# Feed-forward output projections in two halves of the tokens: 256-column matmuls and two evacuations in place of 512-column matmuls and one

## The chip, the cores and the metric

The kernel runs on one core of one Trainium2 chip. The metric is the device time of one execution in microseconds (us), the median of the runs that are shown.

## The reference, cut to what matters

The model is a trunk of two layers on 512 tokens of width 1024, all in float32. Each layer is a half-weighted feed-forward block, a mixer (Mamba-2 SSD in layer 0, S5 in layer 1) and a second half-weighted feed-forward block. The change touches the four feed-forward blocks alone:

```
def swiglu(h, w_in, w_out):
    gate, up = jnp.split(h @ w_in, 2, axis=-1)
    return (jax.nn.silu(gate) * up) @ w_out

x = x + 0.5 * swiglu(rmsnorm(x, ffn1_norm[i]), ffn1_w_in[i], ffn1_w_out[i])
...
x = x + 0.5 * swiglu(rmsnorm(x, ffn2_norm[i]), ffn2_w_in[i], ffn2_w_out[i])
```

`w_in` is 1024 x 5632 and `w_out` 2816 x 1024, so the hidden width is 2816, which is 22 tiles of 128.

## The kernel before, in words

**Layout.** Activations are kept with channels on the partitions and the 512 tokens along the free axis: `xT[d]`, d = 0 to 7, are eight tiles of 128 x 512 in float32. Six stages run one after the other: `f1_0`, `ssd`, `f2_0`, `f1_1`, `s5`, `f2_1`; the four whose names begin with f are the feed-forward blocks.

**Three matmuls per product.** To keep float32 accuracy with the fast matmul type F32R, each operand is split into a rounded part and a rest. Weights go through `load_w` (L186): a DMA into `wst`, a ScalarE cast into `whi` (L194) and a VectorE subtraction into `wlo` (L196). `proj` (L199) then issues three matmuls for each of its contraction tiles, and each of them names its own 128 x 128 stationary block, so each matmul in the profile has a weight load (engine PEld) of its own:

```
for k in range(n):
    PE.matmul(ps, hi[:, k], H[k], start=first and k == 0, stop=False)       # L203
    PE.matmul(ps, hi[:, k], L[k], start=False, stop=False)                  # L204
    PE.matmul(ps, lo[:, k], H[k], start=False, stop=last and k == n - 1)    # L205
```

**A feed-forward stage, `ffn` (L208).** The 22 hidden tiles are worked in three parts of 8, 7 and 7. For each hidden tile of a part, `proj` computes the gate and the up product, each into a PSUM bank of its own (`mm`, 4 banks in turn). VectorE scales both (`gt` L225, `up` L228), ScalarE applies silu (L226), VectorE multiplies (L229), and the result is split again: `ah` by ScalarE (L231), `al` by VectorE (L233). When a part is done, its output projection follows: for each of the eight output tiles d, `proj` contracts the 8 or 7 tiles `ah`, `al` with the weights of that part into one bank, in 24 or 21 matmuls of 512 columns, and one VectorE instruction (L240) adds half of the bank to `xT[d]`. In the third part, `nxt.take(d)` then prepares the operand of the next stage from `xT[d]` (L170, L172, L157, L162). So a stage has 8 x 22 x 3 = 528 matmuls in output projections and the program 2112.

**What sets the order.** In the feed-forward stages a scheduler places the instructions of each engine; each engine then runs its own list in that order and waits at an instruction until its operands are there. In `ssd` and `s5`, TensorE keeps the order in which the code was written. `fill` hands a feed-forward stage small pieces of other work (the set-up of S5), one after each tile. Buffers that the text speaks of: four banks of the name `mm`, four more of the name `aux`, four `wst`, three each of `whi` and `wlo`, eight each of `ah` and `al`.

Of the kernel before, what the change touches and what calls it, by code (L numbers as in the profile page):

```python
# [30 lines left out]
def trunk_kernel(ctx, tc, x, ffn1_norm, ffn1_w_in, ffn1_w_out, mix_norm, ffn2_norm, ffn2_w_in, ffn2_w_out,  # L31
# [31 lines left out]
    # token residues: qsel[t, (c, q)] = (t % 8 == q), kmask[t, k] = (t // 8 == k)  # L63
# [49 lines left out]
    def newton_rsqrt(ps4, n, scale):  # L113
        """rsqrt(ps4*scale + eps) on a small tile of n columns"""
        v = work.tile([128, 16], F32, name="nw_v")[:, :n]
        hv = work.tile([128, 16], F32, name="nw_h")[:, :n]
        y = work.tile([128, 16], F32, name="nw_y")[:, :n]
        a = work.tile([128, 16], F32, name="nw_a")[:, :n]
        V.tensor_scalar(v, ps4, scale, EPS, op0=OP.mult, op1=OP.add)
        V.tensor_scalar(hv, v, -0.5, None, op0=OP.mult)  # L120
        V.tensor_scalar(a.bitcast(I32), v.bitcast(I32), 1, None, op0=OP.logical_shift_right)
        V.tensor_scalar(y.bitcast(I32), a.bitcast(I32), -1, 0x5f3759df, op0=OP.mult, op1=OP.add)
        for _ in range(3):
            V.tensor_tensor(a, y, y, op=OP.mult)
            V.tensor_tensor(a, a, hv, op=OP.mult)
            V.scalar_tensor_tensor(y, a, 1.5, y, op0=OP.add, op1=OP.mult)
        return y

    def compact_sum(accs, p=None, first=True, last=True):
        """[128, 512] tiles -> sum over partitions and tiles, [128 t, 4]"""  # L130
        p = p or aux_ps()
        for i, acc in enumerate(accs):
            for c in range(4):
                for q in range(4):
                    PE.matmul(p[q * 32:(q + 1) * 32, c:c + 1], acc[:, c * 128 + q * 32:c * 128 + q * 32 + 32],  # L135
                              ones[:, 0:1], start=first and i == 0 and c == 0, stop=last and i == len(accs) - 1,
                              skip_group_check=True)
        return p

    def bcast_rows(y4):  # L140
        """[128 t, 4] -> psum [128, 512], the same row on every partition"""
        p = aux_ps()
        for c in range(4):
            PE.transpose(p[:, c * 128:(c + 1) * 128], y4[:, c:c + 1].to_broadcast([128, 128]), ident)
        return p

    class Prep:
        """takes finished x tiles and prepares the operand of the next stage"""
# [37 lines left out]
    def load_w(src, kt, eng=None):  # L186
        """src [kt*128 rows, 128 columns] -> exact hi/lo stationary blocks"""
        st = wpool.tile([128, KD, 128], F32, name="wst", bufs=4)[:, :kt]
        (eng or nc.sync).dma_start(st, src.rearrange("(k p) c -> p k c", p=128))
        return split_w(st, kt)  # L190
# [17 lines left out]
    def ffn(pr, w_in, w_out, nxt, fill=()):  # L208
        fill = list(fill)

        def pop():
            if fill:
                fill.pop(0)()

        with tc.tile_pool(name="ffn", bufs=2) as fp:
            for a, b in PARTS:
                AH, AL = [], []
                for f in range(a, b):
                    pg, pu = mm_ps(), mm_ps()
                    wg = load_w(w_in[:, f * 128:(f + 1) * 128], KD)  # L220
                    proj(pg, wg, pr.H, pr.L)
                    wu = load_w(w_in[:, FF + f * 128:FF + (f + 1) * 128], KD)
                    proj(pu, wu, pr.H, pr.L)
                    gt = fp.tile([128, T], F32, name="gt")
                    V.tensor_tensor(gt, pg, pr.rbc, op=OP.mult)  # L225
                    S.activation(gt, gt, AF.Silu)  # L226
                    up = fp.tile([128, T], F32, name="up")
                    V.tensor_tensor(up, pu, pr.rbc, op=OP.mult)  # L228
                    V.tensor_tensor(up, up, gt, op=OP.mult)  # L229
                    ah = fp.tile([128, T], F32R, name="ah", bufs=8)  # L230
                    S.copy(ah, up)  # L231
                    al = fp.tile([128, T], F32R, name="al", bufs=8)
                    V.tensor_tensor(al, up, ah.bitcast(F32), op=OP.subtract)  # L233
                    AH.append(ah)
                    AL.append(al)
                    pop()
                for d in range(KD):
                    po = mm_ps()
                    proj(po, load_w(w_out[a * 128:b * 128, d * 128:(d + 1) * 128], b - a), AH, AL)
                    V.scalar_tensor_tensor(xT[d], po, 0.5, xT[d], op0=OP.mult, op1=OP.add)  # L240
                    if b == FT:
                        nxt.take(d)
                    pop()
            while fill:
                fill.pop(0)()
        nxt.finish()

# [1 line left out]
    def ssd(pr, nxt):  # L249
        w_in, w_out = ssd_in_proj[0], ssd_out_proj[0]  # L250
        with ExitStack() as es:
            sc = es.enter_context(tc.tile_pool(name="ssdc", bufs=1))
            sp = es.enter_context(tc.tile_pool(name="ssd", bufs=2))
            # dt for the 32 heads, on four quadrants
# [74 lines left out]
            def conv(ct):  # L329
                """conv channel tile ct (of 32), silu'd, feature-major"""  # L330
# [25 lines left out]
            def out_rows(a, b, last=False):  # L356
                """adds the product of inner tiles a..b with their rows of the output weights"""
                for d in range(KD):
                    po = mm_ps()
                    proj(po, load_w(w_out[a * 128:b * 128, d * 128:(d + 1) * 128], b - a), YH[a:b], YL[a:b])  # L360
                    V.tensor_tensor(xT[d], po, xT[d], op=OP.add)
                    if last:
                        nxt.take(d)
                    pop()
# [10 lines left out]
            def scan(g, BT, CT, XS, SZ):  # L375
                """pieces of the scan of one group"""
                st = {}

                def head():
                    # chunk products C.B, token-major operands  # L380
# [47 lines left out]
                def decay(e):  # L428
                    # decays inside the chunks, per head
# [14 lines left out]
                def outp(e):  # L444
                    M = st["M", e]
                    # decay from the states, rows per head pair
# [80 lines left out]
    s5 = {}  # L527

    def s5_setup(pp, part):
        """closures that build the S5 operators in DRAM"""  # L530
        # per 8 groups: input, state-output and in-chunk operators; phase tables
# [13 lines left out]
        def expf(o, src):  # L545
            """exp to float32 accuracy, argument held to [-87, 88]"""
# [36 lines left out]
        def load_bc(i):  # L583
            gs = slice(i * 8, i * 8 + 8)
            # B stacks: [re; im] and [-im; re]
# [5 lines left out]
            # C stacks: [re; im] and [im; re]  # L591
# [9 lines left out]
        def load_d():  # L601
            # skip term
# [13 lines left out]
        def lam():  # L616
# [22 lines left out]
            # expm1(a) = 2t/(1+|t|) * max(1, e^a), t = tanh(a/2)  # L639
# [6 lines left out]
            # powers of lambda_bar, m = 0..8  # L646
# [22 lines left out]
            # c0 = (lambda_bar - 1)/lambda  # L669
# [25 lines left out]
            # |lambda_bar|^8 and the unit phase ^8, conjugated on the lower half  # L695
# [27 lines left out]
            # [re; -re], [-im; -im]  # L723
# [5 lines left out]
        def tables(i):  # L729
            """phase tables for 8 groups: cos, sin of k times the phase of 8 steps"""  # L730
# [18 lines left out]
        def ops(i):  # L749
            """input and output operators of 4 groups"""  # L750
# [82 lines left out]
    def s5_sink(d, g):  # L833
        """x*gain of a finished tile, tokens as (q, k), to DRAM"""
# [10 lines left out]
    def in_ops(i):  # L845
        """tokens of 8 groups, their input operators and tables"""
# [11 lines left out]
    def out_ops(i, h):  # L858
        """output operators of 4 groups"""
        if (i, h) not in s5_out:  # L860
            P_ = s5["op"].tile([128, 4, 256], F32, name="opP", bufs=5)
            nc.sync.dma_start(P_, s5["P"][:, i * 8 + h * 4:i * 8 + h * 4 + 4])
            s5_out[i, h] = P_
        return s5_out[i, h]
# [8 lines left out]
    def res_w(j):  # L873
        """weights kept whole while the scan runs, in the tiles of the next operand"""
# [9 lines left out]
    def s5_stage(pr, nxt):  # L884
        with ExitStack() as es:
            sp = es.enter_context(tc.tile_pool(name="s5", bufs=2))
            # 1/rms in the (c, q) x k layout
# [10 lines left out]
            def scan(i):  # L898
                """states before every chunk, rotated back"""
# [30 lines left out]
            def mix(i, ins, gy):  # L930
                """outputs of tiles i and i + 1, (tile, k) x (g, q, c)"""
# [11 lines left out]
            def channels(i, gy):  # L943
                """back to channels x (q, k)"""
# [169 lines left out]
```

## Time and profile before

| | |
|---|---|
| time, median of 2 runs | 2126.34 us (2125.13 and 2127.54) |
| span of the profiled execution | 2124.6 us |
| TensorE matmul busy | 2055.0 us (97%), 10755 records |
| VectorE busy | 1256.6 us (59%) |
| ScalarE busy | 793.7 us (37%) |
| DMA, mean | 108 GB/s |
| mean granted TensorE clock | 0.987 |

The profiled execution's span is 1.7 us below the median, and what lies around a span is not in it. PE is TensorE's matmul row, PEld its weight loads, which overlap the matmuls; DVE is VectorE, ACT ScalarE, POOL GpSimd, SP the queue that issues most DMAs. A matmul's row gives the time from its start to its modelled end, and the next one starts before that end, so the distance between two starts, not the row's duration, is what a matmul costs in a row of them; below it is called the step. A matmul on plain float32 operands shows as two records in the trace, one of type F32R as one. "L203 PE MATMUL mm<-ah,whi 128*128 128x512" is a matmul at line 203 that writes `mm` from the moving tile `ah` and the stationary tile `whi`, with 512 columns.

### The profile page before, as it was taken

How to read it: one execution, taken by the hardware profiler on the slowest of the kernel's cores; microseconds unless marked ns; L12 is line 12 of the kernel's file. 1: busy time of each engine (PE TensorE's matmuls, PEld its weight loads, DVE VectorE, ACT ScalarE, POOL GpSimd, SP SyncE). 2: the span in 40 equal slices, each digit the busy share in tenths (PEclk: the TensorE clock that was granted, in tenths of full speed). 3: DMA queues.
4: the chain of work that ended last, by engine and by line, in shares of the span. 5: the costliest groups of instructions: out<-in, count | busy, mean ns of one | idle time of the engine just before them, and what ended most of it. 6: DMA issues, size and time to landing. Idle time of an engine off the chain costs nothing.

```text
span 2124.6 us, 27175 instructions
## 1 busy us (share of the span) xinstructions
PE 2055.0 (97%) x10755; PEld 1691.2 (80%) x10755; DVE 1256.6 (59%) x2171; ACT 793.7 (37%) x1146; POOL 44.9 (2%) x116
## 2 busy tenths in 40 slices
PE   6999999999999999699999999999996999999997
PEld 5888888888888887587788888888885788888886
DVE  6887445678875787477844454344457654434444
ACT  4223223566753664243422333232254433222222
POOL 1000000000000001000000000000001000000000
PEclk9999999999999999899999999999998999999999
DMA  5344333322223214756533363333357233332331
GB/s 153 110 130 138 91 99 83 99 74 76 70 72 91 77 41 117 123 148 174 154 95 100 94 201 92 99 96 99 95 159 244 83 100 89 99 100 81 108 92 58
DMA packets 408672, 228.50 MB, mean 108 GB/s; under 512 B 45656, under 2 KB 397072, under 8 KB 408544
## 3 DMA queue, kind: packets, MB, share of 16 engines
q1 hardware_dynamic: 383120, 200.24, 33.1%
q0 software_dynamic: 4272, 13.66, 2.8%
q10 hardware_dynamic: 21152, 12.86, 2.1%
q8 instruction: 84, 1.38, 0.3%
q14 instruction: 44, 0.36, 0.1%
HBM read 204.64 MB, written 22.09 MB: 107 GB/s over the span
## 4 chain that ended last, share of the span: by engine, by line
PE 93%; DVE 3%; DMA 2%; ACT 1%; issue 1%; SPq 0%; POOL 0%; ACTq 0%; DVEq 0%
PE mm L203 29%; PE mm L205 29%; PE mm L204 29%; DMA p_B<-in_s_b_re_dram 1%; PE aux L464 1%; PE aux L414 0%; DVE z L919 0%; PE aux L457 0%; DMA wst<-in_ffn_w_in_dram 0%; PE aux L434 0%; DMA p_lrow<-in_s_lam_re_dram 0%; PE aux L135 0%; PE aux L204 0%; PE aux L205 0%; PE aux L203 0%
## 5 line engine op out<-in xcount | busy, mean ns | idle before, releaser
L194 ACT CAST whi<-wst 128x1024 fp32r<-128x1024 f32 (+2 forms) x357 | 361.1, 1013 | 953.6 <-PE mm L204 676.2
L203 PE MATMUL mm<-hH,whi 128*128 128x512 f32 x1800 | 706.4, 393 | 1.2 <-DVE gt L225 1.2
L205 PE MATMUL mm<-hH,wlo 128*128 128x512 f32 x1800 | 703.5, 391 | 0.0
L204 PE MATMUL mm<-hL,whi 128*128 128x512 f32 x1800 | 703.0, 391 | 0.0
L196 DVE TENSOR_TENSOR wlo<-wst,whi 128x1024 fp32r<-128x1024 f32 (+2 forms) x357 | 418.8, 1174 | 107.9 <-ACT whi L194 104.1
L203 PEld LDWEIGHTS mm<-hH,whi 128*128 128x128 f32 x1800 | 339.2, 189 | 73.1 <-issue 2.0
L205 PEld LDWEIGHTS mm<-hH,wlo 128*128 128x128 f32 x1800 | 338.8, 188 | 71.3 <-issue 0.4
L204 PEld LDWEIGHTS mm<-hL,whi 128*128 128x128 f32 x1800 | 339.1, 188 | 69.8
L204 PE MATMUL mm<-al,whi 128*128 128x512 f32 x704 | 275.8, 392 | 0.0
L205 PE MATMUL mm<-ah,wlo 128*128 128x512 f32 x704 | 275.3, 391 | 0.0
L203 PE MATMUL mm<-ah,whi 128*128 128x512 f32 x704 | 274.9, 391 | 0.0
L228 DVE TENSOR_TENSOR up<-mm,rbc 128x512 f32<-128x512 f32 x88 | 60.7, 690 | 222.2 <-PE mm L205 222.1
L240 DVE SCALAR_TENSOR_TENSOR xT<-mm,xT 128x512 f32<-128x512 f32 x96 | 66.1, 689 | 197.6 <-PE mm L205 197.6
L204 PEld LDWEIGHTS mm<-al,whi 128*128 128x128 f32 x704 | 132.1, 188 | 28.7 <-issue 0.2
L205 PEld LDWEIGHTS mm<-ah,wlo 128*128 128x128 f32 x704 | 132.1, 188 | 28.6 <-issue 0.2
L203 PEld LDWEIGHTS mm<-ah,whi 128*128 128x128 f32 x704 | 132.1, 188 | 28.3
L225 DVE TENSOR_TENSOR gt<-mm,rbc 128x512 f32<-128x512 f32 x88 | 60.7, 690 | 154.8 <-PE mm L205 149.4
L231 ACT CAST ah<-up 128x512 fp32r<-128x512 f32 x88 | 54.8, 623 | 66.3 <-DVE up L229 66.2
L340 DVE SCALAR_TENSOR_TENSOR cv<-raw,cols,cv 128x512 f32<-128x512 f32 x96 | 70.9, 745 | 0.7
L229 DVE TENSOR_TENSOR up<-up,gt 128x512 f32<-128x512 f32 x88 | 60.7, 690 | 7.8 <-ACT gt L226 0.7
L226 ACT ACTIVATE gt<-gt 128x512 f32<-128x512 f32 x88 | 55.1, 627 | 17.0 <-DMA d_P<-p_ks 13.2
L233 DVE TENSOR_TENSOR al<-up,ah 128x512 fp32r<-128x512 f32 x88 | 60.1, 684 | 1.4 <-ACT ah L231 1.4
(333 smaller groups left out, 1726.0 us busy)
## 6 DMA issues: line engine op xcount, KB each, us to landing
wst<-in_ffn_w_in_dram SPq DMA_DIRECT2D x176, 512.0 KB, 3.9
wst<-in_ffn_w_out_dram SPq DMA_DIRECT2D x64, 448.0 KB, 3.7
wst<-in_ssd_in_proj_dram SPq DMA_DIRECT2D x48, 512.0 KB, 4.0
wst<-in_ffn_w_out_dram SPq DMA_DIRECT2D x32, 512.0 KB, 4.2
opP<-d_P SPq DMA_DIRECT2D x16, 512.0 KB, 5.0
wst<-in_s_glu_w_dram POOLq DMA_DIRECT2D x12, 512.0 KB, 5.2
d_t<-p_cs POOLq DMA_DIRECT2D x8, 512.0 KB, 3.0
wst<-in_ssd_out_proj_dram SPq DMA_DIRECT2D x8, 512.0 KB, 4.1
```

Source lines behind the costliest of these rows:

```text
L194: S.copy(hi, st)
L196: V.tensor_tensor(lo, st, hi.bitcast(F32), op=OP.subtract)
L203: PE.matmul(ps, hi[:, k], H[k], start=first and k == 0, stop=False)
L204: PE.matmul(ps, hi[:, k], L[k], start=False, stop=False)
L205: PE.matmul(ps, lo[:, k], H[k], start=False, stop=last and k == n - 1)
L225: V.tensor_tensor(gt, pg, pr.rbc, op=OP.mult)
L226: S.activation(gt, gt, AF.Silu)
L228: V.tensor_tensor(up, pu, pr.rbc, op=OP.mult)
L229: V.tensor_tensor(up, up, gt, op=OP.mult)
L233: V.tensor_tensor(al, up, ah.bitcast(F32), op=OP.subtract)
L240: V.scalar_tensor_tensor(xT[d], po, 0.5, xT[d], op0=OP.mult, op1=OP.add)
L340: V.scalar_tensor_tensor(cv, raw[:, 1 + j:T + 1 + j], col("cw", j * 32 + ct), cv, op0=OP.mult, op1=OP.add)
```

## The change

The output loop of `ffn` loads the weights of an output tile once, as before, and then runs `proj` twice, once for tokens 0 to 255 and once for tokens 256 to 511. Each half has a bank of its own, of which it uses 256 columns, and its own VectorE instruction on 256 columns (now L244). The number of output matmuls goes from 2112 to 4224, of half the columns each, with a weight load each; the number of evacuations from 96 to 192. Weight DMAs and splits, `take`, and the other stages are as before. (The full diff also deletes comments and moves line numbers by 4 behind the loop.)

```
                 for d in range(KD):
-                    po = mm_ps()
-                    proj(po, load_w(w_out[a * 128:b * 128, d * 128:(d + 1) * 128], b - a), AH, AL)
-                    V.scalar_tensor_tensor(xT[d], po, 0.5, xT[d], op0=OP.mult, op1=OP.add)
+                    wo = load_w(w_out[a * 128:b * 128, d * 128:(d + 1) * 128], b - a)
+                    for c in range(2):
+                        cs = slice(c * 256, c * 256 + 256)
+                        po = mm_ps()[:, 0:256]
+                        proj(po, wo, [t_[:, cs] for t_ in AH], [t_[:, cs] for t_ in AL])
+                        V.scalar_tensor_tensor(xT[d][:, cs], po, 0.5, xT[d][:, cs], op0=OP.mult, op1=OP.add)
                     if b == FT:
                         nxt.take(d)
                     pop()
```

**On TensorE,** at the start of the second part's output projection in `f1_0`, the scheduler holds back the product with the last hidden tile, which is finished last, and puts it among the matmuls of a later bank. Before, `mm_2102` is the bank of d = 0 and `mm_2131` that of d = 1; `ah_2098` is the last hidden tile:

```order
L205 MATMUL mm_2131<-ah_1810,wlo_2136 128x512
L203 MATMUL mm_2131<-ah_1882,whi_2134 128x512
L204 MATMUL mm_2131<-al_1884,whi_2134 128x512
L203 MATMUL mm_2102<-ah_2098,whi_2105 128x512
L205 MATMUL mm_2131<-ah_1882,wlo_2136 128x512
```

With the change, `mm_2316` and `mm_2339` are the two halves of d = 0, `mm_2368` is the first half of d = 1, and `ah_2306` is the last hidden tile:

```order
L205 MATMUL mm_2339<-ah_2234,wlo_2314 128x256
L203 MATMUL mm_2368<-ah_1874,whi_2364 128x256
L204 MATMUL mm_2368<-al_1876,whi_2364 128x256
L205 MATMUL mm_2368<-ah_1874,wlo_2366 128x256
L203 MATMUL mm_2368<-ah_1946,whi_2364 128x256
L203 MATMUL mm_2316<-ah_2306,whi_2312 128x256
L203 MATMUL mm_2339<-ah_2306,whi_2312 128x256
```

The first product with the last hidden tile stood behind 29 output matmuls of 512 columns; it now stands behind 40 of 256 columns, and two halves are open at that point instead of one bank.

**On VectorE,** at the same place, the list before and the list with the change read:

```order
L233 TENSOR_TENSOR al_2100<-up_2095,ah_2098 128x512
L240 SCALAR_TENSOR_TENSOR xT0_88<-mm_2102,xT0_88 128x512
L196 TENSOR_TENSOR wlo_2194<-wst_2190,whi_2192 128x896
L240 SCALAR_TENSOR_TENSOR xT1_89<-mm_2131,xT1_89 128x512
L196 TENSOR_TENSOR wlo_2223<-wst_2219,whi_2221 128x896
```

```order
L233 TENSOR_TENSOR al_2308<-up_2303,ah_2306 128x512
L244 SCALAR_TENSOR_TENSOR xT0_88<-mm_2316,xT0_88 128x256
L244 SCALAR_TENSOR_TENSOR xT0_88<-mm_2339,xT0_88 128x256
L196 TENSOR_TENSOR wlo_2470<-wst_2466,whi_2468 128x896
L244 SCALAR_TENSOR_TENSOR xT1_89<-mm_2368,xT1_89 128x256
L244 SCALAR_TENSOR_TENSOR xT1_89<-mm_2391,xT1_89 128x256
L196 TENSOR_TENSOR wlo_2522<-wst_2518,whi_2520 128x896
```

Each evacuation of 512 columns became two neighbours of 256, with one weight split between the pairs as before.

## The prediction

> **What bounds the kernel now.** I read the page's busy times first, then the chain that ended last, then the groups of instructions.
>
> ```profile
> span 2124.6 us, 27175 instructions
> PE 2055.0 (97%) x10755; PEld 1691.2 (80%) x10755; DVE 1256.6 (59%) x2171; ACT 793.7 (37%) x1146; POOL 44.9 (2%) x116
> PE 93%; DVE 3%; DMA 2%; ACT 1%; issue 1%; SPq 0%; POOL 0%; ACTq 0%; DVEq 0%
> L204 PE MATMUL mm<-al,whi 128*128 128x512 f32 x704 | 275.8, 392 | 0.0
> L205 PE MATMUL mm<-ah,wlo 128*128 128x512 f32 x704 | 275.3, 391 | 0.0
> L203 PE MATMUL mm<-ah,whi 128*128 128x512 f32 x704 | 274.9, 391 | 0.0
> L240 DVE SCALAR_TENSOR_TENSOR xT<-mm,xT 128x512 f32<-128x512 f32 x96 | 66.1, 689 | 197.6 <-PE mm L205 197.6
> ```
>
> TensorE is busy for 97% of the span and makes 93% of the chain. The three groups with `ah` and `al` are the output projections, 3 x 704 = 2112 matmuls, and TensorE stood idle for 0.0 us before them. VectorE's evacuation waits for TensorE (197.6 us in all), never the other way round. So the change is priced by the step of an output matmul. The timeline of TensorE at the ends of `f1_0` and `f2_0` gives it:
>
> ```profile
> 391.73 0.39 PE L205 MATMUL mm<-ah,wlo 128*128 128x512 f32 x1
> 392.43 0.40 PE L205 MATMUL mm<-ah,wlo 128*128 128x512 f32 x1
> ...
> 1240.18 0.39 PE L205 MATMUL mm<-ah,wlo 128*128 128x512 f32 x1
> 1240.86 0.39 PE L205 MATMUL mm<-ah,wlo 128*128 128x512 f32 x1
> ```
>
> Three matmuls lie from each L205 to the next: 0.68/3 = 226.7 ns in `f2_0`, 0.70/3 = 233.3 ns in `f1_0`. The busy time by stretches says the same for whole parts (x counts the part and two neighbours), at full clock (1.00):
>
> ```profile
> 238.00:277.30 39.30, 39.30 (x170) 31.55 (x170) 15.55 (x18) 8.46 (x10) 0.00 (x0) 1.00 0.35 100
> 1203.00:1241.10 38.10, 38.10 (x170) 31.55 (x169) 24.14 (x32) 16.70 (x24) 0.00 (x0) 1.00 0.36 102
> ```
>
> **The main term: what half of the columns cost.** No F32R matmul of 256 columns is in this trace. If the whole step is proportional to the columns, two halves cost what one whole did, and the term is nothing. If a piece of the step is fixed, each output matmul adds that piece once. The nearest rows are the float32 matmuls of `ssd`, of 128 and 256 columns with the same 128-column weights; the timeline shows them in runs, the groups give one duration:
>
> ```profile
> 438.67 1.06 PE L384 MATMUL aux<-CT,BT 128*128 128x128 f32 x8
> 439.56 1.04 PE L393 MATMUL aux<-ident,xs 128*128 128x128 f32 x8
> 446.22 1.46 PE L414 MATMUL aux<-wx,btok 128*128 128x256 f32 x6
> ...
> L414 PE MATMUL aux<-wx,btok 128*128 128x256 f32 x48 | 11.7, 379 | 0.0
> L384 PE MATMUL aux<-CT,BT 128*128 128x128 f32 x64 | 8.5, 275 | 0.0
> L393 PE MATMUL aux<-ident,xs 128*128 128x128 f32 x64 | 8.3, 273 | 0.0
> ```
>
> A run of n lasts n - 1 steps and one duration. So L384 has a step of (1060 - 275)/7 = 112 ns, L393 (1040 - 273)/7 = 110 ns and L414 (1460 - 379)/5 = 216 ns. From 128 to 256 columns the step grows by 104 to 106 ns, and what is left at no columns is 216 - 2 x 104 = 8 or 216 - 2 x 106 = 4 ns. That is the fixed piece of a float32 step. If an F32R step has the same, half a matmul costs (226.7 + 4)/2 = 115.4 to (226.7 + 8)/2 = 117.4 ns, and a pair 4 to 8 ns more than the whole. I take the middle, 6 ns, and 2112 x 6 = 12.7 us; the slower step of `f1_0` changes nothing in this difference.
>
> The bounds: nothing below (proportional; a pair cheaper than the whole would need a negative fixed piece), and above, F32R columns at just twice the speed of these float32 records, 0.82/2 = 0.41 ns, so 512 columns take 210 ns and 16.7 ns are fixed: 2112 x 16.7 = 35 us. A reason to stay near the lower rows: duration minus step is 275 - 112 = 163 ns at L384, 379 - 216 = 163 at L414 and, in the `f2_0` part below, 389 - 227 = 162 ns for the F32R matmul. So the F32R step's whole length lies inside the matmul's own flight, as streaming does, and not in a gap between two matmuls.
>
> ```profile
> L204 PE MATMUL mm<-al,whi 128*128 128x512 f32 x56 | 21.8, 389 | 0.0
> ```
>
> The Trainium skill ("TensorE: Matmul & The Clock Gate", section "Back-to-back issue gap") gives a warm step as the columns at 2.4 GHz plus 2.5 ns. For 512 columns that is 215.8 ns where this trace has 226.7, so the measurement decides against its level. Taken only for its fixed piece, the sum by the page would be 2112 x 2.5 = 5.3 us in place of 12.7.
>
> **Weight loads.** There are 2112 more. Today a load starts with the matmul before its own and is hidden under it:
>
> ```profile
> 1240.18 0.19 PEld L203 LDWEIGHTS mm<-ah,whi 128*128 128x128 f32 x1
> 1240.41 0.19 PEld L204 LDWEIGHTS mm<-al,whi 128*128 128x128 f32 x1
> L204 PEld LDWEIGHTS mm<-al,whi 128*128 128x128 f32 x704 | 132.1, 188 | 28.7 <-issue 0.2
> L384 PEld LDWEIGHTS aux<-CT,BT 128*128 128x128 f32 x64 | 8.4, 191 | 0.7
> L393 PEld LDWEIGHTS aux<-ident,xs 128*128 128x128 f32 x64 | 7.3, 141 | 0.0
> ```
>
> 188 ns do not fit under a step of 116 ns. But the loads at L384 last 191 ns too, one to each matmul, and the matmuls there step by 112 ns: the end of one load overlaps the start of the next, and a load holds the array for at most 112 ns. With the shorter loads of L393 (141 ns) the step is 110, so at this rate loads cost about 2 ns, which is in the 4 to 8 above. I price the extra loads at nothing beyond that; the cover is thin (116 against 112), and what follows if it goes is the third rival.
>
> The same page, section "LDWEIGHTS (loading the stationary operand)", puts a load at its columns over 1.2 GHz, an estimated 106.7 ns for 128 columns, which speaks against this change: at 256 columns the load is as long as the streaming. L384's 112 ns agree with it, and by it the sum stays as it is.
>
> **Evacuations.** A 128x256 VectorE instruction that reads a bank takes 413 ns:
>
> ```profile
> L424 DVE TENSOR_TENSOR st<-st,aux 128x256 f32<-128x256 f32 x16 | 6.6, 413 | 0.0
> 117.00:161.90 44.90, 44.90 (x194) 36.05 (x194) 38.80 (x112) 9.01 (x10) 2.14 (x4) 1.00 0.45 141
> ```
>
> So a pair costs 2 x 413 - 689 = 137 ns more, 96 x 0.137 = 13 us of VectorE time. VectorE is busy for 24.14 us of 38.10 in a third part, so TensorE's own matmuls hide it. The thinnest place is the first part of `f1_0` (117 to 161.9 us), where the S5 set-up fills VectorE to 38.80 of 44.90 us, and 8 x 0.137 = 1.1 us come on top.
>
> **Banks.** Four banks `mm` now hold two output tiles instead of four. By the listed order of that first part, 26 matmuls of 256 columns (26 x 0.117 = 3.0 us) lie between the last product into the first bank and the first into the fifth, which takes the same bank again; before it was 29 x 0.233 = 6.8 us. An evacuation needs 0.43 us from the matmul's start (1240.86 above, evacuation at 1241.28) and 0.41 of its own, and one weight split (1.2 us) may stand in front: 2.1 us, still under 3.0. Only where set-up work queues on VectorE can TensorE wait; I allow 1.5 us over the whole program (bounds 0, and 4 us for 1 us in each of four stages).
>
> ```profile
> 1241.28 0.69 DVE L240 SCALAR_TENSOR_TENSOR xT<-mm,xT 128x512 f32<-128x512 f32 x1 [1.41 <-PE mm L205]
> L196 DVE TENSOR_TENSOR wlo<-wst,whi 128x1024 fp32r<-128x1024 f32 x8 | 9.7, 1217 | 0.0
> ```
>
> **The last hidden tile.** `ah` and `al` of a part's last tile come late. The part that starts at 238.06 us has `al` at 241.35; the first product that needs `ah` now stands behind 40 matmuls of 256 columns, so 40 x 0.117 = 4.7 us after the start, later than 3.3. No wait arises.
>
> ```profile
> 238.06 0.40 PE L203 MATMUL mm<-ah,whi 128*128 128x512 f32 x1
> 240.66 0.69 DVE L233 TENSOR_TENSOR al<-up,ah 128x512 fp32r<-128x512 f32 x1
> ```
>
> **Stage ends.** At the end of `f1_1` and of the program, TensorE waits for the last evacuation, which now has 256 columns: 2 x (0.689 - 0.413) = 0.55 us saved. **Sum:** 12.7 + 1.5 - 0.6 = 13.6 us on the profiled span of 2124.6, so 2138 us; the median of the runs shown lies 1.7 us higher, so I forecast 2140 us, 0.6% slower, inside the 2% that a measurement of this kernel can tell from no change.
>
> **Rivals.** *First, proportional steps:* nothing is fixed in an F32R step, a pair costs 0 to 3 ns more, and the time is 2126 + 0 to 6 = 2126 to 2132 us. For it: 389 - 227 equals the float32 difference, so no gap lies between matmuls. Against: the 4 to 8 ns left over in the float32 steps.
>
> *Second, a large fixed piece:* 9 to 19 ns per matmul, 19 to 40 us, so 2146 to 2167 us, about 2155 in the middle. For it: F32R needs 226.7 ns where twice the float32 column speed gives 210. Against: the same flight difference.
>
> *Third, slower by more than 2%: weight loads set the step.* If the load of an F32R matmul must end before that matmul starts, the step is at least the load. At 188 ns a pair costs 376, which is 149 ns more, 2112 x 149 = 315 us, so 2441 us. It decides from a step of 123.4 ns on, where 2112 x 20.1 ns are 42.5 us, 2%; at 130 ns it is 2112 x 33 = 70 us and 2196 us. For it: in the rows above each load starts with the matmul ahead and ends 39 ns before its own, so an end-to-start order was never tested for F32R. Against: L384 and L393, where it is broken at every matmul.
>
> *Faster by over 2%* would need pairs under 206.6 ns, less than 512 columns take by any row, or waits of TensorE to remove, which the groups show at 0.0 us.
>
> **How the numbers follow.** The forecast (pairs 4 to 8 ns dearer, 2133 to 2145 us) has 0.50, the proportional case 0.18, the large fixed piece 0.18, the weight loads 0.12, faster 0.02. The range of 2122 to 2172 us takes the first two rivals in whole and the edge of the third, and leaves out about 0.13. Slower by over 2% (above 2169 us) is the third rival and a tail of the second, 0.14; faster 0.02; within 2% 0.84.
>
> **What would show it.** Right: in the changed profile 4224 output matmuls of 128x256 step by 115 to 118 ns in `f2_0`, TensorE's idle time before them stays near 0, evacuations take about 413 ns, and a part of seven tiles (1203 to 1241 us before) lasts 38.6 to 39.5 us. Wrong: a step of 113, of 120 or of 123 and more points to the first, second or third rival; weight loads that stretch, or idle time of PE before L203 put down to DVE L244, to the loads and the banks.

## The result and the profile after

The changed kernel takes 2147.29 us (median of 2 runs, 2147.16 to 2147.42), the kernel before 2126.34 us: a ratio of 1.0101, 95% interval 1.0082 to 1.0120, so about 1.0% slower. The profiled execution went from a span of 2124.6 us to 2145.6, 21.0 us more. First the page of the changed kernel, its busy times, the shares of its chain and the groups that were shown of before:

```profile
span 2145.6 us, 31579 instructions
PE 2076.9 (97%) x12867; PEld 1800.8 (84%) x12867; DVE 1269.8 (59%) x2267; ACT 792.8 (37%) x1146; POOL 43.6 (2%) x116
PE 93%; DVE 3%; DMA 2%; ACT 1%; issue 1%; SPq 0%; ACTq 0%; DVEq 0%
L205 PE MATMUL mm<-ah,wlo 128*128 128x256 f32 x1408 | 395.5, 282 | 0.0
L204 PE MATMUL mm<-al,whi 128*128 128x256 f32 x1408 | 395.0, 282 | 0.0
L203 PE MATMUL mm<-ah,whi 128*128 128x256 f32 x1408 | 393.4, 282 | 0.0
L204 PEld LDWEIGHTS mm<-al,whi 128*128 128x128 f32 x1408 | 268.2, 191 | 0.4
L244 DVE SCALAR_TENSOR_TENSOR xT<-mm,xT 128x256 f32<-128x256 f32 x192 | 79.8, 422 | 174.2 <-PE mm L205 173.5
```

TensorE's busy time rose from 2055.0 to 2076.9 us, by 21.9, and that is the whole loss: what is left of the span, its idle time, went from 69.6 to 68.7 us. The shares of the chain are as before. Nothing new waits: 0.0 us stand before the output matmuls. So the 4224 matmuls of 256 columns take longer than 2112 of 512 did, while TensorE runs without a gap. The busy times by stretches, over the same parts as in the prediction (x counts the part and a neighbour or two), show where; their clock is 1.00:

```profile
115.83:160.64 44.81, 44.81 (x386) 44.80 (x385) 40.07 (x120) 9.03 (x9) 2.14 (x4) 1.00 0.45 142
236.82:276.02 39.20, 39.20 (x337) 39.20 (x336) 17.08 (x26) 8.37 (x9) 0.00 (x0) 1.00 0.34 100
1207.11:1247.42 40.31, 40.31 (x337) 40.30 (x336) 25.12 (x40) 16.38 (x23) 0.00 (x0) 1.00 0.35 100
1335.87:1381.94 46.07, 46.07 (x386) 46.07 (x384) 17.91 (x26) 9.01 (x9) 0.00 (x0) 1.00 0.31 92
```

The first two are parts of `f1_0`. They lasted 44.90 and 39.30 us before and last 44.81 and 39.20 now, no longer at all. The third is a part of `f2_0` with 336 matmuls, and went from 38.10 to 40.31 us; the fourth is a part of `f2_1` with 384. TensorE's timeline, one line of three (L205), at the ends of an `f1_0` part and of that `f2_0` part gives the step (the last four L205 rows of each, the middle two left out):

```profile
390.24 0.28 PE L205 MATMUL mm<-ah,wlo 128*128 128x256 f32 x1
...
391.29 0.28 PE L205 MATMUL mm<-ah,wlo 128*128 128x256 f32 x1
...
1246.22 0.28 PE L205 MATMUL mm<-ah,wlo 128*128 128x256 f32 x1
...
1247.30 0.28 PE L205 MATMUL mm<-ah,wlo 128*128 128x256 f32 x1
```

Nine matmuls lie from the first to the last row of each half: 1.05/9 = 116.7 ns in `f1_0` and 1.08/9 = 120.0 ns in `f2_0`. In `f1_0` that is just half of the 233.3 ns of before, so a pair costs nothing extra. In `f2_0` a pair takes 240.0 ns where one matmul took 226.7, which is 13.3 ns more, and `f2_1` (46.07/384 = 120.0 ns) and `f1_1` step the same way. A stage has 528 such pairs, so three stages lose 1584 x 13.3 = 21.1 us and the fourth loses nothing: this is the time that was lost.

### The profile page after: what moved, and what is told of

Same layout as the page of the kernel before. It is cut to its first block, busy times and chain, and to the rows that moved or that the text cites. A ratio compares the mean times of both kernels' runs of the same rounds, so it can differ in the third digit from the quotient of the medians.

```text
span 2145.6 us, 31579 instructions
## 1 busy us (share of the span) xinstructions
PE 2076.9 (97%) x12867; PEld 1800.8 (84%) x12867; DVE 1269.8 (59%) x2267; ACT 792.8 (37%) x1146; POOL 43.6 (2%) x116
## 4 chain that ended last, share of the span: by engine, by line
PE 93%; DVE 3%; DMA 2%; ACT 1%; issue 1%; SPq 0%; ACTq 0%; DVEq 0%
PE mm L203 29%; PE mm L205 29%; PE mm L204 29%; DMA p_B<-in_s_b_re_dram 1%; PE aux L468 1%; PE aux L418 0%; DVE z L923 0%; PE aux L461 0%; DMA wst<-in_ffn_w_in_dram 0%; PE aux L438 0%; PE aux L135 0%; PE aux L205 0%; PE aux L204 0%; PE aux L203 0%; PE aux L388 0%
## 5 line engine op out<-in xcount | busy, mean ns | idle before, releaser
L205 PE MATMUL mm<-hH,wlo 128*128 128x512 f32 x1800 | 703.1, 391 | 0.0
L205 PEld LDWEIGHTS mm<-hH,wlo 128*128 128x128 f32 x1800 | 339.1, 188 | 70.9
L205 PE MATMUL mm<-ah,wlo 128*128 128x256 f32 x1408 | 395.5, 282 | 0.0
L204 PE MATMUL mm<-al,whi 128*128 128x256 f32 x1408 | 395.0, 282 | 0.0
L203 PE MATMUL mm<-ah,whi 128*128 128x256 f32 x1408 | 393.4, 282 | 0.0
L204 PEld LDWEIGHTS mm<-al,whi 128*128 128x128 f32 x1408 | 268.2, 191 | 0.4
L205 PEld LDWEIGHTS mm<-ah,wlo 128*128 128x128 f32 x1408 | 268.2, 191 | 0.4 <-issue 0.4
L203 PEld LDWEIGHTS mm<-ah,whi 128*128 128x128 f32 x1408 | 267.0, 191 | 0.6 <-issue 0.2
L244 DVE SCALAR_TENSOR_TENSOR xT<-mm,xT 128x256 f32<-128x256 f32 x192 | 79.8, 422 | 174.2 <-PE mm L205 173.5
```

The costliest lines, as they stand in the source:

```text
L244: V.scalar_tensor_tensor(xT[d][:, cs], po, 0.5, xT[d][:, cs], op0=OP.mult, op1=OP.add)
```

## The experiments

What had to be explained: the same instruction costs half of the whole in one stage, and 13.3 ns a pair more in the others. Four theories were put to the test, the fourth formed only after the first round. *Theory 1:* every F32R matmul carries a fixed piece, and `f1_0` is slow already for a reason of its own. *Theory 2:* the place in memory at which the moving tile starts sets the step. *Theory 3:* below some width the loads of the weights set the step. *Theory 4:* what counts is where the moving tile starts relative to the weights. Their first ground is where the built programs put the tiles (the profile does not show it): `whi`, `wlo` and `hH` start 32 bytes past a multiple of 512, `ah` and `al` 64 bytes past one in `f1_0` and 32 bytes past one in the other three stages, `yh` and `yl` 320. A moving tile is 2048 bytes long and a block of weights 512, so all of one name have the same place within 512 bytes. The stage as such is an unlikely cause: in the kernel before, the 336 gate and up matmuls of `f1_0` between two of its output parts, with moving tiles `hH` and `hL`, take from 161.86 to 238.06 us, a step of 226.8 ns next to output matmuls of 233.3. Ratios are against the kernel before in the same runs: 2126.75 us in the first four experiments, 2126.64 in the last three.

**m1: steps by themselves.** A small kernel runs chains of 24 F32R matmuls with the weights `W` and the moving tiles `M` each at 0 (`wA`, `mA`) or at 32 bytes (`wB`, `mB`) past a multiple of 64, at six widths. Its core:

```diff
+    for n in (512, 384, 256, 192, 128, 64):
+        for w in "AB":
+            for m in "AB":
+                chain(w, m, n)
...
+        for r in range(runs):
+            for k in range(K):
+                wk = W[w][:, at[w] + k * 128:at[w] + k * 128 + 128]
+                PE.matmul(p[:, 0:n], wk, M[m][:, k, at[m]:at[m] + n], start=r == 0 and k == 0,
+                          stop=r == runs - 1 and k == K - 1)
```

> This kernel leaves the model out: it copies x to the output and runs chains of 24 F32R matmuls with nothing else on TensorE, for 512, 384, 256, 192, 128 and 64 columns, each with weights that start 0 (wA) or 32 (wB) bytes past a multiple of 64 and moving tiles that start 0 (mA) or 32 (mB) bytes past one. Theory 1 (a fixed piece of 13.3 ns in every F32R matmul, whatever the addresses): the step is 226.7 ns at 512 and 120.0 at 256 columns in all four combinations, and 66.7 at 128. Theory 2 (the piece depends on where the moving tile starts, as f1_0 with 233.3 and 116.7 ns against the other stages with 226.7 and 120.0 suggests): mB gives 226.7 and 120.0, mA 233.3 and 116.7, and the weights' start changes nothing. Theory 3 (the weight load sets the step once it is no longer well hidden): the step at 256 columns depends on the weights' start, and at 128 and 64 columns it stays at about 110 ns, far over 66.7.

TensorE's timeline of it, a row for a chain of 24:

```profile
36.33 5.75 PE L43 MATMUL mm<-mA,wB 128*128 128x512 f32 x24
41.92 5.73 PE L43 MATMUL mm<-mB,wB 128*128 128x512 f32 x24
...
69.95 2.96 PE L43 MATMUL mm<-mA,wB 128*128 128x256 f32 x24
72.75 3.00 PE L43 MATMUL mm<-mB,wB 128*128 128x256 f32 x24
...
83.61 2.84 PE L43 MATMUL mm<-mB,wB 128*128 128x192 f32 x24
86.28 2.82 PE L43 MATMUL mm<-mA,wA 128*128 128x128 f32 x24
88.94 2.84 PE L43 MATMUL mm<-mB,wA 128*128 128x128 f32 x24
...
105.42 5.31 PE L43 MATMUL mm<-mA,wB 128*128 128x64 f32 x24
110.54 5.31 PE L43 MATMUL mm<-mB,wB 128*128 128x64 f32 x24
```

The step is the time from a chain's start to the next one's, over 24. At 512 columns (41.92 - 36.33)/24 = 232.9 ns, and much the same in all four placements. At 256 columns (72.75 - 69.95)/24 = 116.7 to 118 ns. Between these two widths the step is proportional within a nanosecond or two, which speaks against theory 1. That the placements hardly differ speaks against theory 2 as first stated, by starts modulo 64. At 192 columns the step is (86.28 - 83.61)/24 = 111.3 ns and at 128 it is (88.94 - 86.28)/24 = 110.8, so there is a floor, as theory 3 says, and 256 columns lie above it. The last chains, of 64 columns, step by (110.54 - 105.42)/24 = 213.3 ns, but not because of their width. The first 64-column chain, seen up to 98.0 and up to 98.8 us, and the busy times by stretches show what changed:

```profile
96.97 1.25 PE L43 MATMUL mm<-mA,wA 128*128 128x64 f32 x10
96.97 2.03 PE L43 MATMUL mm<-mA,wA 128*128 128x64 f32 x17
...
97.05:98.80 1.75, 1.75 (x18) 1.75 (x17) 0.29 (x1) 0.00 (x0) 0.00 (x0) 1.00 0.02 5
100.30:105.40 5.10, 5.10 (x25) 5.10 (x26) 0.22 (x1) 0.00 (x0) 0.00 (x0) 0.50 0.00 0
```

Ten matmuls take 1.25 us and 17 take 2.03, so a step is 0.78/7 = 111.4 ns at a granted clock of 1.00; the 213.3 ns belong to a clock of 0.50. The floor is the same at 192, 128 and 64 columns, and at half the clock it is nearly twice as long.

The 226.7 ns of the kernel did not appear at all, though. The reason lay in this kernel's layout: its moving tiles stood 2112 bytes apart, so that their starts moved on by 64 bytes from tile to tile, where the real kernel's stand 2048 apart. Experiment m2 mends that.

**e1: the evacuations alone.** The matmuls stay at 512 columns and each bank is evacuated in two halves:

```diff
-                    V.scalar_tensor_tensor(xT[d], po, 0.5, xT[d], op0=OP.mult, op1=OP.add)
+                    for c in range(2):
+                        cs = slice(c * 256, c * 256 + 256)
+                        V.scalar_tensor_tensor(xT[d][:, cs], po[:, cs], 0.5, xT[d][:, cs], op0=OP.mult, op1=OP.add)
```

> The kernel before with one part of the change alone: 512-column output matmuls into one bank as before, evacuated by two VectorE instructions of 256 columns. If all of the 21 us come from the matmuls' steps, the time stays at 2126 us (ratio 0.999 to 1.001) and VectorE is busy for 13 us more. If the evacuations or the banks' release bring part of it, the time is 2130 us or more.

2126.31 us, ratio 0.9999 (0.9990 to 1.0009). Its page has these rows:

```profile
PE 2055.0 (97%) x10755; PEld 1691.3 (80%) x10755; DVE 1264.1 (60%) x2267; ACT 794.1 (37%) x1146; POOL 44.8 (2%) x116
L242 DVE SCALAR_TENSOR_TENSOR xT<-mm,xT 128x256 f32<-128x256 f32 x192 | 72.4, 419 | 196.6 <-PE mm L205 196.5
```

The doubled evacuations cost no time. On VectorE they cost 7.5 us rather than the 13 expected: 192 x 419 ns are 80.4 us, but the group is busy for only 72.4, so the two halves of a pair, which here come right behind each other, overlap. TensorE's 2055.0 us are those of before. What the change lost, it lost in the matmuls.

**e2: the changed kernel with its tiles moved.** 32 bytes ahead of the tiles of `f2_0`, `f1_1` and `f2_1` put their `ah` and `al` where `f1_0` has them, 64 bytes past a multiple of 512:

```diff
-    def ffn(pr, w_in, w_out, nxt, fill=()):
+    def ffn(pr, w_in, w_out, nxt, fill=(), pad=False):
...
         with tc.tile_pool(name="ffn", bufs=2) as fp:
+            if pad:
+                fp.tile([128, 8], F32, name="pad", bufs=1)
...
-                ffn(pr, wi[L], wo[L], nxt)
+                ffn(pr, wi[L], wo[L], nxt, pad=s != "f1_0")
```

> The changed kernel with 32 bytes left free ahead of the tiles of the feed-forward pool in f2_0, f1_1 and f2_1, so that ah and al start at a multiple of 64 bytes there too, as they do in f1_0 (gt and up move with them). Theory 2: the 3168 output matmuls of these stages step by 116.7 ns in place of 120.0, 3168 x 3.33 ns = 10.6 us less, so about 2137 us, ratio to the kernel before 1.005. Theories 1 and 3: the step stays at 120.0 and the time at 2147 us, ratio 1.010.

2138.61 us, ratio 1.0054 (1.0041 to 1.0066): 8.7 us less than the changed kernel, where 10.6 were expected; TensorE's busy time is 10.0 us less (2066.9 for 2076.9). The same part of `f2_0`, first by stretches:

```profile
1205.72:1244.91 39.19, 39.19 (x337) 39.19 (x336) 25.14 (x40) 16.40 (x23) 0.00 (x0) 1.00 0.35 100
```

and in the timeline:

```profile
1243.75 0.28 PE L205 MATMUL mm<-ah,wlo 128*128 128x256 f32 x1
...
1244.80 0.28 PE L205 MATMUL mm<-ah,wlo 128*128 128x256 f32 x1
```

It steps by 1.05/9 = 116.7 ns now: 32 bytes of unused memory took 3.3 ns from each matmul of this width. So theory 1, a piece that is fixed whatever the addresses, falls in the real kernel too, and the place counts. Against before, a pair costs 233.3 - 226.7 = 6.7 ns, 1584 x 6.7 = 10.6 us; measured are 11.9.

**e3: four quarters in place of two halves.**

```diff
-                    for c in range(2):
+                    for c in range(4):
...
-                        cs = slice(c * 256, c * 256 + 256)
-                        po = mm_ps()[:, 0:256]
+                        cs = slice(c * 128, c * 128 + 128)
+                        po = mm_ps()[:, 0:128]
```

> The changed kernel with four quarters of 128 columns in place of two halves. Theories 1 and 2 with loads hidden: a step of 66.7 ns, so four cost 266.7 ns where the whole cost 226.7, 2112 x 40 = 84 us more than before, 2211 us. Theory 3: a load of 128 columns holds the array for about 110 ns, four steps cost 440 ns, 2112 x 213 = 450 us more than before, about 2576 us, and the weight-load row is busy without gaps.

2587.73 us, ratio 1.2167 (1.2144 to 1.2189). A group of the page's weight loads, and a part of seven tiles by stretches:

```profile
L205 PEld LDWEIGHTS mm<-ah,wlo 128*128 128x128 f32 x2816 | 540.0, 192 | 0.0
```

```profile
1396.01:1470.89 74.88, 74.88 (x673) 74.87 (x671) 27.84 (x56) 16.37 (x23) 0.00 (x0) 1.00 0.19 55
```

672 matmuls of 128 columns fill 74.88 us: a step of 111.4 ns, hardly less than at 256 columns. Four of them cost 4 x 111.4 = 445.6 ns where one of 512 columns cost 226.7, so 2112 x 219 = 462 us; measured are 461. The floor of theory 3 decides at this width, and theories 1 and 2 (2211 us) have none. That the loads set the floor is not shown by this: a load's row lasts 192 ns, longer than the step, so the loads overlap. From the proportional step of `f1_0` and e2, 116.7/256 = 0.456 ns a column, the floor of 111.4 ns would be reached at an estimated 244 columns: the change stopped just above it.

**m2: steps by the tiles' places.** The small kernel again, with moving tiles 2048 bytes and blocks of weights 512 bytes apart, as in the real one. The moving tiles start at 0 to 448 bytes past a multiple of 512, the weights at 32 (lines 47 to 56) or at 0 (lines 59 to 61):

```diff
+        for n in (512, 256):
+            for m, mm in w32_m.items():
+                run(mm, 32, m, n)
+            for m, mm in w0_m.items():
+                run(mm, 0, m, n)
...
+                mm(p[:, 0:n], W[:, w0 + k * 128:w0 + k * 128 + 128], M[:, m0 + k * 512:m0 + k * 512 + n],
+                   start=r == 0 and k == 0, stop=r == runs - 1 and k == K - 1)
```

> This kernel leaves the model out: it copies x to the output and runs chains of 24 F32R matmuls of 512 and then of 256 columns, with tiles 2048 bytes apart as in the kernel; lines 47 to 56 take weights that start 32 bytes past a multiple of 512 and moving tiles that start 0, 32, 64, 96, 128, 192, 256, 320, 384 and 448 bytes past one, lines 59 to 61 weights at 0 with moving tiles at 0, 32 and 64. Theory 4 (the step depends on whether moving tile and weights start at the same place within 512 bytes, as they do in the stages with 226.7 and 120.0 ns, both 32 past, and not in f1_0, 64 against 32): 226.7 and 120.0 ns at lines 48 and 59, about 233 and 117 ns at all others. Theory 2 in its first form (only the moving tile's start past a multiple of 64 counts): 226.7 and 120.0 at lines 48, 50 and 60. If the steps are alike in all lines, the cause lies in what runs beside the matmuls.

TensorE's timeline, a row for a chain of 24; the line tells the place (L47: moving tile at 0, weights at 32; L48: both at 32; L49: 64 and 32; L50: 96 and 32; L51: 128 and 32; L54: 320 and 32; L55: 384 and 32; L59: both at 0; L60: 32 and 0; L61: 64 and 0):

```profile
36.21 5.63 PE L48 MATMUL mm<-mv,wt 128*128 128x512 f32 x24
41.67 5.77 PE L49 MATMUL mm<-mv,wt 128*128 128x512 f32 x24
47.27 5.67 PE L50 MATMUL mm<-mv,wt 128*128 128x512 f32 x24
52.78 5.77 PE L51 MATMUL mm<-mv,wt 128*128 128x512 f32 x24
...
86.42 5.65 PE L59 MATMUL mm<-mv,wt 128*128 128x512 f32 x24
91.90 5.77 PE L60 MATMUL mm<-mv,wt 128*128 128x512 f32 x24
97.51 5.67 PE L61 MATMUL mm<-mv,wt 128*128 128x512 f32 x24
103.01 3.00 PE L47 MATMUL mm<-mv,wt 128*128 128x256 f32 x24
105.85 3.04 PE L48 MATMUL mm<-mv,wt 128*128 128x256 f32 x24
108.72 3.00 PE L49 MATMUL mm<-mv,wt 128*128 128x256 f32 x24
...
122.94 2.97 PE L54 MATMUL mm<-mv,wt 128*128 128x256 f32 x24
125.74 3.04 PE L55 MATMUL mm<-mv,wt 128*128 128x256 f32 x24
128.62 3.02 PE L56 MATMUL mm<-mv,wt 128*128 128x256 f32 x24
131.47 3.04 PE L59 MATMUL mm<-mv,wt 128*128 128x256 f32 x24
134.35 3.00 PE L60 MATMUL mm<-mv,wt 128*128 128x256 f32 x24
137.18 2.99 PE L61 MATMUL mm<-mv,wt 128*128 128x256 f32 x24
```

At 512 columns the chains with both at one place last 5.46 and 5.48 us (L48: 41.67 - 36.21; L59: 91.90 - 86.42), about 228 ns a step. Those 64 bytes apart in L50 and L61 take 5.51 and 5.50, about 229.4, an intermediate value that theory 4 did not foresee. All others, among them L49 and L60 with 32 bytes between, take 5.60 to 5.62, about 233.5. The theory's main line holds at 512 columns: tiles at one place step fastest. Theory 2 does not: a moving tile at 32 is quick with weights at 32 (L48) and slow with weights at 0 (L60). At 256 columns the order turns round: both at one place makes 2.87 and 2.88 us (120 ns), and 32 bytes apart (L47, L60, and L49 too) 2.83 to 2.84 (118). Here the theory is not clean: L55, 352 bytes apart, takes 2.88 too, and the quickest, L54 at 2.80 (116.7 ns), is 288 bytes apart. Nor do these chains give the 116.7 ns that the kernel has at 32 bytes between (`f1_0`, e2), so at this width something besides the place within 512 bytes counts too.

**e4: the kernel before, with `f1_0` moved by 32 bytes.** The edit of e2, made on the kernel before and for `f1_0` alone (`pad=s == "f1_0"`), puts its tiles 96 bytes past a multiple of 512, 64 from the weights.

```diff
         with tc.tile_pool(name="ffn", bufs=2) as fp:
+            if pad:
+                fp.tile([128, 8], F32, name="pad", bufs=1)
...
-                    ffn(pr, wi[L], wo[L], nxt, fill=s5_setup(pp, s5_pre.index(s)))
+                    ffn(pr, wi[L], wo[L], nxt, fill=s5_setup(pp, s5_pre.index(s)), pad=s == "f1_0")
```

> The kernel before with 32 bytes left free ahead of the feed-forward tiles of f1_0 alone: ah and al there start 96 bytes past a multiple of 512 in place of 64, so 32 past a multiple of 64 as in the other stages, but not at the weights' place within 512. Theory 2: the 528 output matmuls of f1_0 step by 226.7 in place of 233.3 ns, 3.5 us less, 2123 us. Theory 4: they stay at 233 ns and the time at 2126 us.

2123.07 us, ratio 0.9984 (0.9975 to 0.9993). The timeline of `f1_0`:

```profile
388.63 0.39 PE L205 MATMUL mm<-ah,wlo 128*128 128x512 f32 x1
...
390.00 0.39 PE L205 MATMUL mm<-ah,wlo 128*128 128x512 f32 x1
```

The row between them is left out: 1.37/6 = 228.3 ns, and 229.0 over the part: the intermediate step of L50 and L61 in m2, and between the 226.7 ns of tiles at one place and the 233.3 ns that theory 4 gives any other. 528 x 4.3 = 2.3 us are expected from it, and 3.6 were measured with an interval of 1.5 to 5.3. The time is the one that theory 2 gave (2123 us), but its step of 226.7 ns is not there: the time alone would have misled.

**e5: the kernel before, all output tiles where the weights start.** In e4's edit the spare tile becomes 480 bytes, and one of 224 bytes goes ahead of the tiles of `ssd`, so that `ah`, `al`, `yh` and `yl` all start 32 bytes past a multiple of 512:

```diff
         with tc.tile_pool(name="ffn", bufs=2) as fp:
+            if pad:
+                fp.tile([128, 120], F32, name="pad", bufs=1)
...
             sp = es.enter_context(tc.tile_pool(name="ssd", bufs=2))
+            sp.tile([128, 56], F32, name="pad2", bufs=1)
```

> The kernel before with 480 bytes left free ahead of the feed-forward tiles of f1_0 and 224 ahead of those of ssd, so that ah, al, yh and yl all start 32 bytes past a multiple of 512, as the weights do. Theories 2 and 4: 528 output matmuls of f1_0 and 384 of ssd step by 226.7 in place of 233.3 ns, 912 x 6.7 = 6.1 us less, 2120 us, ratio 0.997, faster than both kernels. If the step has to do with the stage and not the addresses, 2126 us.

2121.15 us, ratio 0.9973 (0.9963 to 0.9983), faster than both kernels. The busy times of its page and its timeline in `f1_0`:

```profile
PE 2049.9 (97%) x10755; PEld 1692.0 (80%) x10755; DVE 1256.5 (59%) x2171; ACT 793.5 (37%) x1146; POOL 45.2 (2%) x116
```

```profile
387.69 0.39 PE L205 MATMUL mm<-ah,wlo 128*128 128x512 f32 x1
388.37 0.39 PE L205 MATMUL mm<-ah,wlo 128*128 128x512 f32 x1
```

0.68/3 = 226.7 ns: `f1_0` now steps as the other stages do, without any change to its work, and so does the output projection of `ssd` (L205 at 829.63, 830.31 and 830.99 us). 528 + 384 matmuls x 6.7 ns are 6.1 us; TensorE's busy time fell by 5.1 and the median by 5.5.

## Why the prediction was right, and where not

**What bounds it** held. TensorE's busy time grew by 21.9 us and the span by 21.0, and no other engine entered the chain. The sign and the verdict (within 2%) were right, and the 2147 us lie inside the range. They lie 7 us above the forecast, though, and past the forecast's own 2133 to 2145 us; the range held them because it was drawn to take in the second rival, not because the main term was right.

**The main term is the one mis-sized.** A fixed piece of 6 ns, taken from float32 steps, was to cost each of 2112 pairs, 12.7 us. Measured are 13.3 ns in 1584 pairs and 0 in 528, 21.1 us or 10 ns on the mean. The step that failed is the reading of `f1_0`: "the slower step of `f1_0` changes nothing in this difference". Both its price and the price of the others depend on where the tiles start, and the two steps, 226.7 and 233.3, were the first sign of it. The stage with the slow step was the one that halved without loss (e2 shows the same at 116.7 ns), and the stages with the quick step fell to 120.0. There is no one fixed piece for all F32R matmuls; the float32 rows, taken at the one place that each has, could not show that. By the signs that the prediction set, the step of 120 and the seven-tile part of 40.31 us (38.6 to 39.5 were forecast) point to the second rival.

**The bounds, 0 to 35 us,** held the 21.1. The argument that the lower rows are nearer, since duration less step is 162 to 163 ns in both formats, did not carry: 282 - 120 is 162 ns as well, so that difference, which rests on a modelled end, says nothing on the size of a fixed piece.

**Weight loads** set no step, as priced: their rows of 191 ns follow each other without a gap, and the steps of 116.7 to 120 ns stay above the floor. Whether the loads have a part in what the place costs is open, since the step depends on where the moving tile starts relative to the weights. The floor is real: 111.4 ns in e3 against the 112 ns read from L384. That the two are so close is luck in part, because L384's step follows its columns (112 ns at 128, L414's 216 at 256) and only bounds what a load can take. The cover was as thin as the prediction said (116.7 to 120 against 111.4). The rule of the Trainium skill weighed there ("TensorE: Matmul & The Clock Gate", section "LDWEIGHTS (loading the stationary operand)") gives an estimated 106.7 ns for a load, and the measured floor lies 5 ns above it. The same page's section "Back-to-back issue gap", by whose rule for the warm step 256 columns would take an estimated 109.2 ns, falls short of the 116.7 to 120.0 measured.

**Evacuations:** 422 ns where 413 were predicted, and VectorE's busy time rose by 13.2 us where 13 were; hidden, as e1 shows for 96 pairs on their own. **Banks, the last hidden tile and the stage ends** were to give 1.5, 0 and -0.6 us. Idle time before the output matmuls is 0.0 us, and TensorE's idle time in all fell by 0.9, so the 1.5 us for banks was too much.

**The rivals.** The first (proportional) describes `f1_0` exactly and the rest not at all. The second's window, 2146 to 2167 us, holds the result, and its 9 to 19 ns hold the 13.3 of three stages; its reason, a piece fixed in every F32R matmul, fell in m1 and e2. For tiles at one place alone it does fit. The kernel before ran some `f1_0` matmuls at a granted clock of 0.50:

```profile
49.68 0.63 PE L204 MATMUL mm<-hL,whi 128*128 128x512 f32 x1
...
53.95 0.63 PE L205 MATMUL mm<-hH,wlo 128*128 128x512 f32 x1
...
49.00:54.00 5.00, 4.92 (x12) 3.86 (x13) 4.97 (x14) 2.48 (x4) 0.00 (x0) 0.50 0.36 106
```

Ten steps take 4.27 us, 427 ns each. If all of that went with the clock, 512 columns would take 213.5 ns at full clock, and 256 would take 106.8. At one place the measured steps, 226.7 and 120.0, both lie 13.2 ns above this, a fixed piece; in `f1_0` the steps, 233.3 and 116.7, lie 19.8 and 9.9 above it, a piece that goes with the columns. This is an estimate from two widths, and no run tried a third at one place. The third rival would have decided from a step of 123.4 ns and did not. With quarters a floor does decide, but not by that rival's rule, that a load must end before its matmul starts: the loads there last 192 ns and the step is 111.4.

**What stays open.** Why one place is quick at 512 columns and slow at 256 is not settled. Nor is which bits of the addresses count: 64 bytes between the tiles gives 229 ns at 512 columns, and at 256 columns several distances beside 0 come near 120. What sets the floor of 111 ns was not taken apart either. It does not go with the moving columns (192, 128 and 64 step alike in m1), and a limit on matmuls per time is an unlikely cause: 64 float32 matmuls with weights of 32 columns (L135) take 0.71 us in all in the trace of the kernel before, from 514.91 us on. The 128-column loads are what the F32R chains have in common, but no run changed them alone.

## What to carry to other kernels

Before an operand is cut, look whether the same instruction already has two steps in different stages, and find out why: here 6.7 ns in 226.7, which the prediction set aside, told that the price of the cut depends on placement. F32R matmuls with 128-column weights had a shortest useful width here, an estimated 244 columns, and a cut that ends near it has no cover left. Before a longer step is put down to an instruction's shape, look at the granted clock of that stretch (the 64-column chains of m1). A few hundred bytes of padding are worth a try where TensorE is the bound: they brought 5.5 us here (e5), and the change itself cost 21.

## What the runs showed of the hardware

- The step of an F32R matmul depends on where the moving tile starts relative to the weights. At 512 columns it is 226.7 ns with both at the same place within 512 bytes, 229 with 64 bytes between, and 233.3 at the other distances tried (m2, e4, e5). At 256 columns it is 120.0 at the same place, and with 32 bytes between 116.7 in the real kernel (e2) and 118 in the small one (m2).
- With weights of 128 columns, F32R matmuls of 192, 128 and 64 columns step alike, by 111 ns at a granted clock of 1.00 (m1, e3). At 0.50 the 64-column chains step by 213 ns (m1).
- At a granted clock of 0.50 an F32R matmul of 512 columns steps by 427 ns, where it takes 226.7 at 1.00 with the same tiles (the kernel before).
